# A third tile for keys, output weights loaded one group ahead, and one zero instead of a tile of zeros

## The chip, the core and the metric

The kernel runs on one core of one Trainium2 chip. The metric is the device time of one execution in microseconds (us). The names of the engines are those of the profile: PE multiplies matrices, DVE does elementwise work and scans, ACT evaluates functions, POOL does small elementwise work, SP issues transfers (DMA). Each engine takes its instructions in the order in which they were written into its queue; a scheduler wrote that order when the kernel was built, from the order of the program and an estimated timeline.

## The reference, cut to what matters

```python
# T = 2048 rows, D = 1024, 8 heads of 64, 8 gating groups of 64, D_FF = 4096
h = rmsnorm(x, norm_mix_g)
q, k, v, u, vg = split(h @ w_in)              # 5 x 512 columns
# stick-breaking attention, for each query t and key s < t (else 0):
z = q @ k.T / 8
a[t, s] = sigmoid(z[t, s]) * prod(1 - sigmoid(z[t, j]) for s < j < t)
a_out = a @ v
b_out = spatial_gating(gelu(u), gelu(vg), ...)
mix = concat(rmsnorm(a_out), rmsnorm(b_out))
x = x + mix @ w_out
h = rmsnorm(x, norm_mlp_g)
x = x + square(relu(h @ w_up)) @ w_down
return rmsnorm(x, norm_final_g)
```

## The kernel before

The 2048 rows are worked on in 4 chunks of 512 (`c` = 0 to 3). Every matrix product is made of three matmuls of split operands (`mm3`, L93 to L95: high x high, high x low, low x high); `split` (L85, L86) makes the two halves, a copy on ACT and a subtraction on DVE. Below, such a matmul is called a main matmul.

Attention is a generator of 320 steps. A unit is a chunk of queries, a head and a segment of 512 keys (1, 2, 3, 4 segments for chunks 0 to 3); it has 4 steps of 128 queries. A step has three parts. `weigh` makes the scores: two matmuls into `z` (three in a segment on the diagonal, where they are also narrower), two sigmoids on ACT (`kk`, `b`), a scan on DVE along the keys (`pr`, L385, or L382 on the diagonal) and a product on DVE (`b`, L386 or L383). `turn`, 5 steps later, transposes `b` on PE (`tr`, four transposes, or 4 to 1 in the steps of a diagonal unit) and splits the result into `aT`. `gather`, 2 steps after that, multiplies with the values (`av`, two matmuls); at the end of a head, `low` and `ao` add the halves, and every second head `ao` is stored to `a_d`.

Keys (`kt`, 2 tiles) and values (`vt`, 3 tiles) of a unit are loaded by SP at its first step; a load waits there until an earlier unit gives its tile back, and what stands behind it on SP waits as well.

The attention steps run beside other work: the projections of chunks 2 and 3, then for chunks 0, 1 and 2 the class `Out`, then `up_plain` (the up projection of chunks 0 and 1, between `Out(1)` and `Out(2)`) and `down_plain` (behind `Out(2)`). `together` sets how many steps go with a piece of main work. Attention of a chunk must have ended before its `Out` begins.

`Out` has three parts. `operands` loads the gating output (`b_d`, L499) and the attention output (`a_d`, L501), transposes the first on PE (L514), splits both, and sums squares of the second with 32 matmuls by a column of ones (L524, below called the ones). `product` has 192 main matmuls in 4 groups of 48 (`group(half, part, ...)`), each with a pair of weight tiles from `wo_d` (L532), and adds each result into rows of x (`ys`) on DVE (L555). `turn` normalises the rows (L574, L576) and transposes them (L581). The pair for group (0, 1) is loaded in `operands`; each other pair where its group begins:

```python
def group(half, part, m, rr):
    ws = self.ready.pop() if self.ready else self.weights(half, part)
```

The tiles named `t` come from one pool of 14 (`rm.t8`), which `Out`, `up_plain` and `down_plain` share. `zeros` is a tile of 513 columns of zeros: the scan adds it (L382, L385), and POOL copies from it into a part of `aT` (L401).

Of the kernel before, what the change touches and what calls it, by code (L numbers as in the profile page):

```python
# [8 lines left out]
F32 = mybir.dt.float32  # L9
F32R = mybir.dt.float32r  # L10
BF16 = mybir.dt.bfloat16
AF = mybir.ActivationFunctionType
ALU = mybir.AluOpType
# [3 lines left out]
P = 128  # L17
# [3 lines left out]
HD = 64  # L21
SBW = 512
DFF = 4096
TC = 512
# [10 lines left out]
def block_kernel(ctx: ExitStack, tc: tile.TileContext, x, x_t, gmix, w_in, ln_g, ln_b, sgw, sgb,  # L35
                 outg, w_out, gmlp, w_up, w_down, gfin, out):
    nc = tc.nc
# [34 lines left out]
    wo_d = dram.tile([2, 2, 2, P, 4, 512], F32, name="wo_d")  # L72
# [268 lines left out]
    def attention(cs):  # L341
# [4 lines left out]
        def weigh(u, tb):  # L346
# [4 lines left out]
            if tb == 0:  # L351
                kt = att.tile([P, 2, TC], F32R, name="kt", bufs=2)
# [4 lines left out]
                if diag:  # L357
                    qt = att.tile([P, TC], F32R, name="qt", bufs=2)
                    nc.sync.dma_start(qt.bitcast(F32), q_d[h].rearrange("x d t -> (x d) t")[:, tcs])
                    carry = [None] * NTB  # L360
# [20 lines left out]
            if diag:  # L381
                nc.vector.tensor_tensor_scan(pr[:, L - 1::-1], kk[:, L - 1::-1], zeros[:, :L], 1.0, ALU.mult, ALU.add)  # L382
                nc.vector.tensor_tensor(b[:, :L - 1], b[:, :L - 1], pr[:, 1:L], ALU.mult)  # L383
            else:
                nc.vector.tensor_tensor_scan(pr[:, ::-1], kk[:, ::-1], zeros, carry[tb], ALU.mult, ALU.add)  # L385
                nc.vector.tensor_tensor(b, b, pr[:, 1:TC + 1], ALU.mult)  # L386
# [3 lines left out]
        def turn(u, j):  # L390
# [8 lines left out]
            if t0 > TC - 2 * P:  # L399
                t0 = TC - 2 * P  # L400
                nc.gpsimd.tensor_copy(aT[:, :, t0:t0 + P], zeros[:, :2 * P].rearrange("p (a b) -> p a b", a=2))  # L401
# [4 lines left out]
        def gather(u, j):  # L406
# [14 lines left out]
            low = att.tile([HD, TC], F32, name="low", bufs=1)  # L421
            nc.scalar.activation(low, av[HD:2 * HD, :], AF.Copy)
            o0 = (h % 2) * HD
            nc.vector.tensor_tensor(ao[o0:o0 + HD, :], av[0:HD, :], low, ALU.add)
# [63 lines left out]
    class Out:  # L488
# [5 lines left out]
        def operands(self):  # L494
            rm, c = self.rm, self.c
            self.rbs = []
            self.ready = [self.weights(0, 1)]
# [31 lines left out]
        def weights(self, half, part):  # L529
            w = self.rm.pair([4, 512])  # L530
            for i in range(2):
                nc.sync.dma_start(w[i].bitcast(F32), wo_d[half, part, i])  # L532
            return w

        def product(self):
# [9 lines left out]
            def group(half, part, m, rr):  # L545
                ws = self.ready.pop() if self.ready else self.weights(half, part)
# [13 lines left out]
            yield from group(0, 1, self.bm, self.rbs)  # L560
            yield from group(0, 0, self.am, self.ras)
            yield from group(1, 1, self.bm, self.rbs)
            yield from group(1, 0, self.am, self.ras)
# [424 lines left out]
    with ExitStack() as es:  # L988
# [4 lines left out]
        zeros = att.tile([P, TC + 1], F32, name="zeros")  # L993
# [96 lines left out]
```

## Time and profile before

| what | value |
|---|---|
| time, median of 3 runs | 2500.56 us (2498.76 to 2502.59) |
| the profiled execution | 2500.81 us |
| its span, first to last instruction | 2499.1 us |
| mean granted clock of PE | 0.985 of full speed |
| busy PE, DVE, ACT, POOL | 97%, 67%, 48%, 13% of the span |

Busy is time in which an engine executes; the granted clock 1.0 is 2.4 GHz and 0.5 is 1.2 GHz, and a value between is a mean over a stretch in which both occurred. A window of the profile gives the busy time of each engine in a stretch of the span; what an engine lacks to the length of the window is its idle time there.

### The profile page before, as it was taken

The page shows a single profiled execution, that of the slowest core. Times are in us where ns is not written, and L with a number is a line of the kernel's source. Part 1 is how long each engine was busy: PE and PEld are TensorE (multiplying, and loading weights), DVE is VectorE, ACT ScalarE, POOL GpSimd, SP SyncE. Part 2 cuts the span into 40 slices and gives each one's busy share as a digit, 9 for nine tenths or more (in the row PEclk, how much of TensorE's full clock was granted, in tenths as well). Part 3 has the DMA queues.
Part 4 walks back from the last instruction along what each step waited for, and adds up shares of the span by engine and source line. Part 5 has one row for each costly group of instructions (what it writes and reads, how often), then busy time and mean ns, then how long its engine had stood idle before and what let it go on. Part 6 is the DMA issues. An engine that isn't in the chain of part 4 may idle for free.

```text
span 2499.1 us, 30545 instructions
## 1 busy us (share of the span) xinstructions
PE 2427.0 (97%) x11424; PEld 1986.8 (79%) x11424; DVE 1686.5 (67%) x2264; ACT 1197.9 (48%) x2004; POOL 322.1 (13%) x288
## 2 busy tenths in 40 slices
PE   8999999998899999999999899999999999899998
PEld 7888788886687888888877688888888888688886
DVE  4752678865957666666668878744686666577788
ACT  5433457553736655655655545322244444433333
POOL 1110011000100000000000000000123222224432
PEclk9999999998999999999989999999999999999999
DMA  9788977668644334433364543353533444744422
GB/s 378 295 303 280 316 256 247 200 217 282 199 148 143 119 125 131 122 115 111 124 257 170 176 130 113 105 197 126 211 118 139 155 146 163 260 182 153 168 101 101
DMA packets 161108, 455.00 MB, mean 182 GB/s; under 512 B 13376, under 2 KB 29760, under 8 KB 141504
## 3 DMA queue, kind: packets, MB, share of 16 engines
q1 hardware_dynamic: 150320, 417.39, 49.3%
q0 software_dynamic: 6336, 33.56, 3.3%
q10 hardware_dynamic: 4304, 2.10, 0.3%
q8 instruction: 90, 1.47, 0.2%
q14 instruction: 58, 0.48, 0.1%
HBM read 322.97 MB, written 130.02 MB: 181 GB/s over the span
## 4 chain that ended last, share of the span: by engine, by line
PE 83%; DVE 8%; DMA 4%; issue 3%; ACT 2%; POOL 0%; SPq 0%; DVEq 0%; POOLq 0%; ACTq 0%
PE mm L94 23%; PE mm L95 23%; PE mm L93 23%; PE tr L396 4%; PE av L414 2%; PE av L415 2%; PE z L370 2%; PE z L371 2%; DVE w L86 2%; DMA v_d<-qkv_st 1%; DVE pr L385 1%; DMA w_in<-wi_d 1%; PE mm L524 1%; DVE t L86 1%; DVE aT L86 1%
## 5 line engine op out<-in xcount | busy, mean ns | idle before, releaser
L93 PE MATMUL mm<-t,t 128*128 128x512 f32 x1280 | 503.7, 395 | 1.4 <-DVE t L86 1.4
L95 PE MATMUL mm<-t,t 128*128 128x512 f32 x1280 | 503.1, 393 | 0.0
L94 PE MATMUL mm<-t,t 128*128 128x512 f32 x1280 | 501.8, 392 | 0.0
L377 ACT ACTIVATE kk<-z,rq 128x512 f32<-128x512 f32 (+2 forms) x320 | 201.7, 631 | 289.0 <-PE z L371 177.0
L385 DVE TENSOR_TENSOR_SCAN pr<-kk,pr,zeros 128x513 f32<-128x513 f32 x192 | 246.6, 1285 | 119.1 <-ACT kk L377 118.7
L93 PEld LDWEIGHTS mm<-t,t 128*128 128x128 f32 x1280 | 242.3, 189 | 52.0 <-DVE t L86 1.9
L95 PEld LDWEIGHTS mm<-t,t 128*128 128x128 f32 x1280 | 241.7, 189 | 51.8
L94 PEld LDWEIGHTS mm<-t,t 128*128 128x128 f32 x1280 | 242.0, 189 | 50.1
L85 ACT ACTIVATE aT<-tr 128x512 fp32r<-128x512 f32 (+1 forms) x320 | 172.1, 541 | 100.2 <-PE tr L396 99.5
L86 DVE TENSOR_TENSOR aT<-tr,aT 128x512 fp32r<-128x512 f32 (+1 forms) x320 | 190.7, 599 | 25.3 <-ACT aT L85 25.2
L396 PE MATMUL tr<-ident,b 128*128 128x128 f32 x1088 | 180.9, 279 | 24.2 <-DVE aT L86 21.9
L379 ACT ACTIVATE b<-z,rq 128x512 f32<-128x512 f32 (+2 forms) x320 | 201.0, 629 | 2.8 <-PE tr L396 2.7
L85 ACT ACTIVATE t<-t 128x1024 fp32r<-128x1024 f32 x104 | 104.5, 1059 | 170.4 <-DMA t<-in_w_down 101.3
L94 PE MATMUL mm<-w,w 128*128 128x512 f32 x448 | 176.3, 393 | 8.8 <-DVE w L86 8.6
L396 PEld LDWEIGHTS tr<-ident,b 128*128 128x128 f32 x1088 | 133.2, 143 | 60.7 <-DVE aT L86 30.4
L95 PE MATMUL mm<-w,w 128*128 128x512 f32 x448 | 175.1, 391 | 0.0
L85 ACT ACTIVATE w<-raw 128x512 fp32r<-128x512 f32 (+1 forms) x135 | 106.7, 802 | 140.4 <-PE mm L95 130.7
L382 DVE TENSOR_TENSOR_SCAN pr<-kk,zeros 128x128 f32<-128x128 f32 (+3 forms) x128 | 104.4, 818 | 92.0 <-ACT kk L377 91.8
L86 DVE TENSOR_TENSOR w<-raw,w 128x512 fp32r<-128x512 f32 (+1 forms) x135 | 149.9, 1112 | 0.9 <-ACT w L85 0.4
L95 PE MATMUL mm<-t,w 128*128 128x512 f32 x380 | 150.3, 396 | 0.0
L93 PE MATMUL mm<-t,w 128*128 128x512 f32 x380 | 150.2, 395 | 0.0
L94 PE MATMUL mm<-t,w 128*128 128x512 f32 x380 | 150.2, 395 | 0.0
(215 smaller groups left out, 4730.8 us busy)
## 6 DMA issues: line engine op xcount, KB each, us to landing
w_in<-wi_d SPq DMA_DIRECT2D x40, 1024.0 KB, 8.5
kt<-k_d SPq DMA_DIRECT2D x160, 256.0 KB, 5.0
t<-wo_d SPq DMA_DIRECT2D x32, 1024.0 KB, 8.9
t<-in_w_down SPq DMA_DIRECT2D x28, 1024.0 KB, 7.1
raw<-s_d SPq DMA_DIRECT2D x28, 1024.0 KB, 4.8
wi_d<-w_in POOLq DMA_DIRECT2D x20, 1024.0 KB, 10.3
vt<-v_d SPq DMA_DIRECT2D x80, 256.0 KB, 2.7
t<-in_w_up SPq DMA_DIRECT2D x16, 1024.0 KB, 7.6
```

What stands on the lines that cost most here:

```text
L85: nc.scalar.activation(hi, src, AF.Copy)
L86: nc.vector.tensor_tensor(lo, src, hi.bitcast(F32), ALU.subtract)
L93: nc.tensor.matmul(ps, lh, rh, start=first, stop=False, skip_group_check=more)
L94: nc.tensor.matmul(ps, lh, rl, start=False, stop=False, skip_group_check=more)
L95: nc.tensor.matmul(ps, ll, rh, start=False, stop=last, skip_group_check=more)
L370: nc.tensor.matmul(z[:, :Z], ql, kt[:, 0, :Z], start=True, stop=False)
L371: nc.tensor.matmul(z[:, :Z], ql, kt[:, 1, :Z], start=False, stop=not diag)
L377: nc.scalar.activation(kk[:, :L], z[:, :L], AF.Sigmoid, scale=rq[:, 1, row:row + 1])
L379: nc.scalar.activation(b[:, :L], z[:, :L], AF.Sigmoid, scale=rq[:, 0, row:row + 1])
L382: nc.vector.tensor_tensor_scan(pr[:, L - 1::-1], kk[:, L - 1::-1], zeros[:, :L], 1.0, ALU.mult, ALU.add)
L385: nc.vector.tensor_tensor_scan(pr[:, ::-1], kk[:, ::-1], zeros, carry[tb], ALU.mult, ALU.add)
L396: nc.tensor.transpose(tr[:, tb * P:(tb + 1) * P], bs[tb][:, j * P:(j + 1) * P], ident)
```

## The change

Keys get three tiles instead of two. To make room, the tile of zeros becomes one column, which the scan and POOL read again and again, and the tile `low` goes: ACT copies the lower half of the sum straight to its place in `ao`, and DVE adds to it there. In `Out`, the weights of a group are loaded where the group before it begins, and each of these loads keeps its place in the order of the program on SP, so that it stands behind every transfer that the program issues earlier; before, the scheduler could move it ahead.

```diff
-                kt = att.tile([P, 2, TC], F32R, name="kt", bufs=2)
+                kt = att.tile([P, 2, TC], F32R, name="kt", bufs=3)
...
-                nc.vector.tensor_tensor_scan(pr[:, L - 1::-1], kk[:, L - 1::-1], zeros[:, :L], 1.0, ALU.mult, ALU.add)
+                nc.vector.tensor_tensor_scan(pr[:, L - 1::-1], kk[:, L - 1::-1], zeros.broadcast_to([P, L]), 1.0, ALU.mult, ALU.add)
...
-                nc.vector.tensor_tensor_scan(pr[:, ::-1], kk[:, ::-1], zeros, carry[tb], ALU.mult, ALU.add)
+                nc.vector.tensor_tensor_scan(pr[:, ::-1], kk[:, ::-1], zeros.broadcast_to([P, TC + 1]), carry[tb], ALU.mult, ALU.add)
...
-                nc.gpsimd.tensor_copy(aT[:, :, t0:t0 + P], zeros[:, :2 * P].rearrange("p (a b) -> p a b", a=2))
+                nc.gpsimd.tensor_copy(aT[:, :, t0:t0 + P], zeros.unsqueeze(2).broadcast_to([P, 2, P]))
...
-            low = att.tile([HD, TC], F32, name="low", bufs=1)
-            nc.scalar.activation(low, av[HD:2 * HD, :], AF.Copy)
             o0 = (h % 2) * HD
-            nc.vector.tensor_tensor(ao[o0:o0 + HD, :], av[0:HD, :], low, ALU.add)
+            nc.scalar.activation(ao[o0:o0 + HD, :], av[HD:2 * HD, :], AF.Copy)
+            nc.vector.tensor_tensor(ao[o0:o0 + HD, :], av[0:HD, :], ao[o0:o0 + HD, :], ALU.add)
...
-            self.ready = [self.weights(0, 1)]
+            self.ready = []
+            self.weights(0, 1)
...
-                nc.sync.dma_start(w[i].bitcast(F32), wo_d[half, part, i])
-            return w
+
+                tc.keep_in_program_order(nc.sync.dma_start(w[i].bitcast(F32), wo_d[half, part, i]))
+            self.ready.append(w)
...
-            def group(half, part, m, rr):
-                ws = self.ready.pop() if self.ready else self.weights(half, part)
+            def group(half, part, m, rr, then):
+                for hp in then:
+                    self.weights(*hp)
+                ws = self.ready.pop(0)
...
-            yield from group(0, 1, self.bm, self.rbs)
-            yield from group(0, 0, self.am, self.ras)
-            yield from group(1, 1, self.bm, self.rbs)
-            yield from group(1, 0, self.am, self.ras)
+            yield from group(0, 1, self.bm, self.rbs, [(0, 0)])
+            yield from group(0, 0, self.am, self.ras, [(1, 1)])
+            yield from group(1, 1, self.bm, self.rbs, [(1, 0)])
+            yield from group(1, 0, self.am, self.ras, [])
...
-        zeros = att.tile([P, TC + 1], F32, name="zeros")
+        zeros = att.tile([P, 1], F32, name="zeros")
```

With this the scheduler writes another order on all engines. Three places of it follow; a row is the line, the operation, what it writes and reads, and its shape, and `x2` stands for two such rows in a run. From L418 on the lines of the changed kernel have other numbers (L532 became L533, L555 became L558, L634 became L637).

First SP, where `up_plain` ends and `Out(2)` begins. Before (`t` are the pool's tiles, `act_d` takes the last results of the up projection):

```order
L356 DMA vt<-v_d 128x512
L354 DMA kt<-k_d 64x2x512 x2
L532 DMA t_11441<-wo_d 128x2048
L532 DMA t_11442<-wo_d 128x2048
L499 DMA t_11445<-b_d 128x4x512
L356 DMA vt<-v_d 128x512
L501 DMA t_11447<-a_d 128x4x512
L354 DMA kt<-k_d 64x2x512 x2
L634 DMA act_d_98<-t_11158 128x1024
L634 DMA act_d_99<-t_11158 128x1024
L356 DMA vt<-v_d 128x512
L354 DMA kt<-k_d 64x2x512 x2
```

Of the change:

```order
L356 DMA vt<-v_d 128x512
L354 DMA kt<-k_d 64x2x512 x2
L637 DMA act_d_98<-t_11132 128x1024
L356 DMA vt<-v_d 128x512
L637 DMA act_d_99<-t_11132 128x1024
L533 DMA t_11414<-wo_d 128x2048
L533 DMA t_11415<-wo_d 128x2048
L499 DMA t_11418<-b_d 128x4x512
L501 DMA t_11420<-a_d 128x4x512
L354 DMA kt<-k_d 64x2x512 x4
L359 DMA qt<-q_d 128x512
L356 DMA vt<-v_d 128x512
```

The two `wo_d` loads, `b_d` and `a_d` stood ahead of the last two stores to `act_d` and now stand behind both; four loads of `kt` stand behind them in a run.

Then DVE at the start of the product of `Out(2)`. Before (L555 adds a result of 12 main matmuls into `ys`; `SCALAR_TENSOR_TENSOR pr` is the scan; the other rows but L77 are attention's):

```order
L77 TENSOR_SCALAR ra_m<-mm 128x4
L555 SCALAR_TENSOR_TENSOR t_11573<-mm,rb,t_11573 128x512 x2
L555 SCALAR_TENSOR_TENSOR t_11575<-mm,rb,t_11575 128x512
L86 TENSOR_TENSOR aT<-tr,aT 128x512
L555 SCALAR_TENSOR_TENSOR t_11575<-mm,rb,t_11575 128x512
L385 SCALAR_TENSOR_TENSOR pr<-kk_1875,pr,zeros 128x513
L386 TENSOR_TENSOR b<-b,pr 128x512
L86 TENSOR_TENSOR aT<-tr,aT 128x512
L555 SCALAR_TENSOR_TENSOR t_11573<-mm,ra_r,t_11573 128x512
L382 SCALAR_TENSOR_TENSOR pr<-kk_1877,zeros 128x128
L383 TENSOR_TENSOR b<-b,pr 128x127
L86 TENSOR_TENSOR aT<-tr,aT 128x512
```

Of the change:

```order
L386 TENSOR_TENSOR b<-b,pr 128x512
L77 TENSOR_SCALAR ra_m<-mm 128x4
L558 SCALAR_TENSOR_TENSOR t_11546<-mm,rb,t_11546 128x512 x2
L558 SCALAR_TENSOR_TENSOR t_11548<-mm,rb,t_11548 128x512 x2
L558 SCALAR_TENSOR_TENSOR t_11546<-mm,ra_r,t_11546 128x512 x2
L558 SCALAR_TENSOR_TENSOR t_11548<-mm,ra_r,t_11548 128x512 x2
L558 SCALAR_TENSOR_TENSOR t_11546<-mm,rb,t_11546 128x512 x2
L558 SCALAR_TENSOR_TENSOR t_11548<-mm,rb,t_11548 128x512
L86 TENSOR_TENSOR aT<-tr,aT 128x384
L423 TENSOR_TENSOR ao<-av,ao 64x512
L558 SCALAR_TENSOR_TENSOR t_11548<-mm,rb,t_11548 128x512
L385 SCALAR_TENSOR_TENSOR pr<-kk_1879,pr,zeros 128x513
```

Eleven additions of the product now run without an attention step between them; before, one or more rows of attention stood behind the third and behind each later one.

Last DVE at the start of the product of `Out(0)`. Before:

```order
L77 TENSOR_SCALAR ra_m<-mm 128x4
L555 SCALAR_TENSOR_TENSOR t_5289<-mm,rb,t_5289 128x512 x2
L555 SCALAR_TENSOR_TENSOR t_5291<-mm,rb,t_5291 128x512 x2
L555 SCALAR_TENSOR_TENSOR t_5289<-mm,ra_r,t_5289 128x512 x2
L555 SCALAR_TENSOR_TENSOR t_5291<-mm,ra_r,t_5291 128x512 x2
L555 SCALAR_TENSOR_TENSOR t_5289<-mm,rb,t_5289 128x512 x2
L555 SCALAR_TENSOR_TENSOR t_5291<-mm,rb,t_5291 128x512
L385 SCALAR_TENSOR_TENSOR pr<-kk_1879,pr,zeros 128x513
L386 TENSOR_TENSOR b<-b,pr 128x512
L555 SCALAR_TENSOR_TENSOR t_5291<-mm,rb,t_5291 128x512
L385 SCALAR_TENSOR_TENSOR pr<-kk_1875,pr,zeros 128x513
L386 TENSOR_TENSOR b<-b,pr 128x512
```

Of the change:

```order
L385 SCALAR_TENSOR_TENSOR pr<-kk_1877,pr,zeros 128x513
L386 TENSOR_TENSOR b<-b,pr 128x512
L385 SCALAR_TENSOR_TENSOR pr<-kk_1879,pr,zeros 128x513
L86 TENSOR_TENSOR aT<-tr,aT 128x384
L386 TENSOR_TENSOR b<-b,pr 128x512
L423 TENSOR_TENSOR ao<-av,ao 64x512
L86 TENSOR_TENSOR aT<-tr,aT 128x256
L77 TENSOR_SCALAR ra_m<-mm 128x4
L558 SCALAR_TENSOR_TENSOR t_5276<-mm,rb,t_5276 128x512 x2
L558 SCALAR_TENSOR_TENSOR t_5278<-mm,rb,t_5278 128x512 x2
L558 SCALAR_TENSOR_TENSOR t_5276<-mm,ra_r,t_5276 128x512 x2
L558 SCALAR_TENSOR_TENSOR t_5278<-mm,ra_r,t_5278 128x512 x2
```

Four pairs of scan and product that stood among the additions (L385 and L386; two of the pairs are in the first excerpt) now stand ahead of the first addition, two of them in the second excerpt, and with them three rows of `aT`.

## Rows read from the trace of the kernel before

**Rows 1.** Part 1 of the page: busy us of each engine, share, instructions.

```profile
PE 2427.0 (97%) x11424; PEld 1986.8 (79%) x11424; DVE 1686.5 (67%) x2264; ACT 1197.9 (48%) x2004; POOL 322.1 (13%) x288
```

**Rows 2.** Waits of PE: total us, times, longest us.

```profile
PE tr L396 <- DVE aT L86: 21.9, 21, 3.7
PE av L414 <- DMA vt<-v_d: 1.7, 1, 1.7
PE z L370 <- DMA kt<-k_d: 0.4, 1, 0.4
```

**Rows 3.** Windows: length, busy of each engine, PEclk, DMA share, GB/s.

```profile
558.50:591.97 33.47, 23.48 (x123) 16.94 (x122) 28.95 (x49) 25.98 (x54) 3.33 (x5) 0.90 0.99 313
647.20:689.74 42.54, 31.25 (x162) 23.11 (x160) 42.01 (x65) 36.70 (x72) 5.72 (x7) 0.88 0.80 263
1276.00:1295.19 19.19, 15.49 (x74) 13.08 (x73) 17.57 (x23) 13.86 (x23) 0.00 (x0) 0.68 0.89 331
1295.19:1357.00 61.81, 61.81 (x293) 50.91 (x293) 39.53 (x56) 22.39 (x42) 3.42 (x4) 0.96 0.36 127
1357.00:1397.16 40.16, 28.26 (x146) 20.39 (x145) 37.44 (x51) 31.25 (x57) 2.81 (x3) 0.89 1.02 329
1397.16:1450.00 52.84, 52.84 (x241) 43.54 (x241) 38.13 (x47) 20.54 (x29) 0.00 (x0) 0.98 0.32 101
```

**Rows 4.** SP's issues in time order: start, us until issued.

```profile
650.70 0.43 SPq L499 DMA_DIRECT2D t<-b_d  x1
1251.30 0.42 SPq L499 DMA_DIRECT2D t<-b_d  x1
1269.24 7.12 SPq L634 DMA_DIRECT2D act_d<-t  x2
```

**Rows 5.** DVE by form: count, busy us, mean ns, idle before.

```profile
L385 DVE TENSOR_TENSOR_SCAN pr<-kk,pr,zeros 128x513 f32<-128x513 f32 x192 | 246.6, 1285 | 119.1 <-ACT kk L377 118.7
L386 DVE TENSOR_TENSOR b<-b,pr 128x512 f32<-128x512 f32 x192 | 132.0, 688 | 12.4 <-DVE pr L385 0.9
L86 DVE TENSOR_TENSOR aT<-tr,aT 128x512 fp32r<-128x512 f32 x224 | 152.0, 680 | 23.2 <-ACT aT L85 23.2
L86 DVE TENSOR_TENSOR aT<-tr,aT 128x384 fp32r<-128x384 f32 x32 | 17.4, 545 | 0.6 <-ACT aT L85 0.5
L86 DVE TENSOR_TENSOR aT<-tr,aT 128x256 fp32r<-128x256 f32 x32 | 13.2, 412 | 0.0
L424 DVE TENSOR_TENSOR ao<-av,low 64x512 f32<-64x512 f32 x32 | 21.7, 679 | 2.8 <-ACT low L422 2.2
L289 DVE TENSOR_TENSOR vn<-mm,sgb_t 128x256 f32<-128x256 f32 x24 | 8.9, 413 | 0.4 <-PE mm L286 0.4
```

**Rows 6.** DVE by line, the four widths of a line together.

```profile
L382 DVE TENSOR_TENSOR_SCAN pr<-kk,zeros 128x128 f32<-128x128 f32 (+3 forms) x128 | 104.4, 818 | 92.0 <-ACT kk L377 91.8
L383 DVE TENSOR_TENSOR b<-b,pr 128x127 f32<-128x127 f32 (+3 forms) x128 | 62.3, 489 | 9.6 <-ACT t L520 0.3
```

**Rows 7.** Chain that ended last, 645 to 700 us: start, us, what.

```profile
663.41 0.60 DVE b L386
664.01 0.60 DVE aT L86
664.61 1.19 DVE pr L385
```

**Rows 8.** PE in time order near 688 us: start, busy us.

```profile
688.02 0.40 PE L414 MATMUL av<-aT,vt 128*128 128x512 f32 x1
688.25 0.40 PE L370 MATMUL z<-kt,qt 128*128 128x512 f32 x1
688.49 0.39 PE L371 MATMUL z<-kt,qt 128*128 128x512 f32 x1
688.72 0.60 PE L396 MATMUL tr<-ident,b 128*128 128x128 f32 x4
689.07 0.47 PE L415 MATMUL av<-aT,vt 128*128 128x512 f32 x1
```

## The prediction

> **What bounds the kernel now.** Part 1 of the page comes first: PE is busy for 2427.0 of 2499.1 us, so some 72 us of idle PE is all that a better order could win, and whatever makes PE idle costs its full length [rows 1]. The waits of PE say who makes it idle. The longest wait among the attention steps is transposes for a split on DVE, 21.9 us; waits for loaded values come to 1.7 us, and for keys to 0.4 us, once [rows 2]. No row of that view has PE waiting for `wo_d`. So the two loads that the change speeds up stand in nobody's way.
>
> Next I looked at where PE is idle, by windows. Around each `Out` there is a stretch in which the program has no main matmuls ready and PE works through attention steps alone. I call it bare. There are four: ahead of the product of `Out(0)` (558.5 to 591.97 us), of `Out(1)` (647.2 to 689.74) and of `Out(2)` (1276 to 1295.19), and ahead of `down_plain` (1357 to 1397.16). In them PE is idle 9.99, 11.29, 3.70 and 11.90 us, together 36.9, while DVE is busy for 28.95 of 33.47, 42.01 of 42.54, 17.57 of 19.19 and 37.44 of 40.16 us [rows 3]. In a bare stretch DVE sets the pace. In the windows behind, where steps lie between main matmuls, PE is busy from end to end and DVE only in part: 39.53 of 61.81 us in the product of `Out(2)`, 38.13 of 52.84 at the start of `down_plain` [rows 3]. There a step costs PE's time for its own matmuls and DVE's part is free.
>
> **The third tile, the zeros, `low`.** An earlier load of keys can take away the 0.4 us, nothing more; I count 0, bounds -0.4 and 0 [rows 2]. The scan with one zero read again is not in the trace. The nearest row is L289, which reads a column again and again and takes 413 ns, against 412 ns for L86 of the same 256 columns with two full operands [rows 5]; so I take 0 for the scan, and a rival has the other value. POOL copies the same 256 columns as before, and POOL is 13% busy [rows 1]; 0, hidden behind the steps between turn and gather. Without `low`, ACT and DVE do the same two instructions for a head; only the wait for the store of `ao` moves from DVE to ACT. Bounds 0 and one such addition, 0.68 us, for a head that ends in a bare stretch [rows 5]; 0.
>
> **The weights and what moves with them.** `wo_d` loads keep their place on SP, and `b_d` and `a_d` follow them. Before, `b_d` for `Out(2)` was issued at 1251.30 us, while `up_plain` still ran; now it stands behind both last stores to `act_d`, which were issued from 1269.24 us until 7.12 us later [rows 4]. For `Out(1)` it was issued at 650.70 us [rows 4]; now it stands behind a key tile that needs the scores of attention step 108, ten steps into the bare stretch. Behind them four loads of keys stand in a run, as the order of SP shows, which the third tile allows. With the operands late, the scheduler lets more attention steps run first. Counted in PE's order, the scores of this many steps stand ahead of the first main matmul behind each bare stretch, before and now: 92 and 96; 115 and 118; 255 and 263; 282 and 287 (here ahead of the fourth main matmul, before the fourth having come 2 steps after the first). At the beginning of each stretch the counts agree, and they agree again when the product, or the first part of `down_plain`, is done. Twenty steps lose their cover of main matmuls.
>
> **Price on DVE.** DVE's order ahead of the first addition behind each stretch has, more than before: for `Out(0)` 4 scans, 4 products and splits of 512, 384 and 256 columns, 4 x 1.285 + 4 x 0.688 + 0.680 + 0.545 + 0.412 = 9.5 us; for `Out(1)` 3 scans, 5 products, splits of 3 x 512, 384 and 256 and one addition into `ao`, 3.86 + 3.44 + 2.04 + 0.96 + 0.68 = 11.0; for `Out(2)` 4 full scans, 4 diagonal ones at 0.818, 4 products at 0.489, 4 at 0.688 and 8 splits, 5.14 + 3.27 + 1.96 + 2.75 + 5.44 = 18.6; for `down_plain` 5 scans, 3 products and a split, 9.2 [rows 5, 6]. The sum is 48.2 us. Those means contain overlap with the next instruction: in the chain a product, a split and a scan follow each other in 0.60 + 0.60 + 1.19 = 2.39 us [rows 7], against 2.65 us by the means, 0.90 of it. That makes 43.4 us.
>
> Some of it fits into DVE's idle time in the four windows, 4.52 + 0.53 + 1.62 + 2.72 = 9.4 us [rows 3]. Much of that idle time is DVE waiting for its turn in a chain through PE and ACT, so I let half be filled, 4.7 us; bounds 0 and 9.4.
>
> **Price given back on PE.** The same steps no longer take PE time among the main matmuls. At full clock a 512-column attention matmul comes 0.23 to 0.24 us after the one before, and four transposes take 0.35 us [rows 8]. Moved, place by place, are 8, 6, 16 and 10 score matmuls (8 of the 16 are diagonal, some narrower; I take them all at 0.24 and leave out their four short masks), 6, 17, 32 and 4 transposes, and 0, 8, 15 and 2 value matmuls, counted in PE's order: 2.4 + 4.8 + 10.1 + 3.2 = 20.5 us back.
>
> **The sum.** 43.4 - 4.7 - 20.5 = +18.2 us. Its bounds: 43.4 - 9.4 - 20.5 = +13.5 and 48.2 - 20.5 = +27.7. The profiled execution took 2500.8 us, 1.7 more than its span and 0.2 more than the median of the runs, so the forecast is 2519 us, from 2514 to 2528.5. The granted clock is 0.68 to 0.89 in the bare stretches and 0.96 to 0.98 behind them [rows 3]: of the two levels the lower (1.2 GHz) is met there, after DVE has kept PE waiting. Longer bare stretches do not change what DVE needs, so I add nothing; main matmuls that start at the lower level are in both kernels.
>
> The Trainium skill, in Perfetto Trace Analysis, Optimization Strategy, says that a kernel whose most loaded engine changes over time may gain by interleaving its regimes. The windows agree (DVE full in the bare stretches, PE full behind them), and this change separates the regimes further; the page gives no size, so by it the time would rise by an amount that only the rows tell.
>
> **Rivals.** *The loads themselves come too late.* For `Out(1)`, ten steps at 2.39 us put the issue of `b_d` at 671 us or later. In the old run the first main matmul came 43.5 us after that issue (694.2 against 650.70). If all of that were in series, it would come at 714.7, where the sum above has 694.2 + 0.90 x 11.0 - 0.3 = 703.8: 11 us more, 2530. Against it: that time was filled with attention on DVE, not with waiting.
>
> *The pulled steps hide behind the ones.* The 32 one-column matmuls L524 need nothing of DVE, and DVE works through what is queued. In the third window PE is busy with them to its end at 1295.19 while DVE has 1.62 us left [rows 3]. If in each of the four places another 4.5 us of pulled DVE work ran behind PE's own, 18 us would be covered: 2501, no change. Against it: transposes ahead of the ones wait for DVE, and most of the pulled work is theirs.
>
> *The scan gets cheaper with one column of zeros.* The other side: a scan costs 1285 ns for 513 columns, a product of two tiles 688 [rows 5]. If the second operand is what costs the difference, each scan saves up to 0.5 us on average, and the bare stretches hold 72 steps now (13, 18, 6 and 15 before, counted in PE's order, and the 20): -36 us, 2483. It decides from 0.25 us a scan on (18.2 / 72). Against it: L289 saves nothing.
>
> *More tiles remove the gaps.* Repeated gaps in front of the same instructions would mean that tiles of keys run out; with a third all 36.9 us of idle PE in the bare stretches [rows 3] would go, and the steps pulled ahead would be the ones that now can run: 2464. Against it: the row for keys has 0.4 us [rows 2]. The Trainium skill, in Perfetto Trace Analysis, Optimization Strategy, has this reading of a gap that keeps coming back; the waits here do not bear it out.
>
> **How the numbers follow.** Chances: the forecast 0.68, loads too late 0.10, hidden behind the ones 0.14, cheaper scan 0.05, more tiles 0.03. Within 0.2% (5 us) is about what a measurement of this kernel can tell from no change. Slower by more than that: 0.68 + 0.10 = 0.78; same 0.14; faster 0.08. The range holds the forecast's bounds and the late loads; as the cases below them hold 0.22, it takes in the upper part of the hidden case too: 2505 to 2531.
>
> **What would show it.** In the changed profile the four bare stretches are longer by some 6, 10, 16 and 7 us with DVE busy throughout, the products behind them shorter by some 2, 5, 10 and 3; PE's waits for DVE's splits grow by 10 to 20 us in all; the waits for keys were and stay under 1 us; scans take 1.28 us. The prediction is wrong if DVE shows idle time in longer bare stretches (loads late), if the stretches did not grow, or if the mean of L385 moved.

## The result and the profile after

The changed kernel took 2520.3 us, median of 4 runs (2515.7 to 2523.5), against 2499.7 us (2498.1 to 2502.6) for the kernel before on the same chip: 1.008 times, 95% interval 1.0061 to 1.0098. The forecast was 2519. The profiled execution took 2515.7 us, 14.9 more than the profiled one of before; it is the fastest of the four, so what is read from it place by place adds up to 14.9 and not to the 20.6 of the medians.

The page's part 1, the line that answers to [rows 1]:

```profile
PE 2433.5 (97%) x11424; PEld 1987.6 (79%) x11424; DVE 1684.1 (67%) x2264; ACT 1198.5 (48%) x2004; POOL 325.1 (13%) x288
```

PE is busy for 6.5 us more with the same number of instructions, and the span grew by 14.9, so 8.4 us are idle time of PE. The mean granted clock of PE is 0.984, before 0.985. PE's waits, as in [rows 2] (total, times, longest):

```profile
PE tr L396 <- DVE aT L86: 30.4, 32, 2.2
...
PE z L370 <- ACT b L379: 6.9, 8, 1.9
...
PE av L414 <- ACT t L85: 2.1, 1, 2.1
...
PE mm L95 <- DVE w_in L86: 0.9, 1, 0.9
...
PE mm L514 <- DMA t<-b_d: 0.6, 1, 0.6
...
PE z L370 <- DMA kt<-k_d: 0.3, 1, 0.3
```

Transposes wait 8.5 us more for DVE's splits, in 32 places instead of 21; the forecast had 10 to 20 us. Keys cost 0.3 us instead of 0.4, and `b_d`, which is issued later, 0.6. The windows that answer to [rows 3], each from the same point of the program to the same point (length, busy of each engine, PEclk, DMA share, GB/s); second and fourth are the products of `Out(0)` and `Out(1)`, which stood at 49.83 and 56.68 us:

```profile
562.78:598.96 36.18, 26.73 (x137) 18.97 (x136) 35.24 (x57) 30.76 (x62) 2.55 (x6) 0.91 0.97 293
602.70:649.98 47.28, 47.28 (x211) 39.22 (x211) 17.32 (x28) 3.52 (x9) 2.12 (x3) 0.97 0.50 178
649.98:701.89 51.91, 40.03 (x193) 30.00 (x192) 51.33 (x77) 43.51 (x84) 9.22 (x8) 0.80 0.71 199
706.28:757.74 51.46, 51.46 (x229) 42.52 (x230) 22.47 (x33) 7.16 (x15) 2.11 (x3) 0.95 0.48 158
1283.06:1318.83 35.77, 26.43 (x143) 20.22 (x142) 34.60 (x51) 28.92 (x55) 2.80 (x4) 0.91 0.93 315
1318.83:1369.49 50.66, 50.66 (x225) 41.69 (x226) 21.07 (x30) 9.75 (x18) 2.51 (x4) 0.96 0.34 132
1369.49:1413.74 44.25, 30.89 (x168) 22.17 (x166) 43.18 (x60) 37.05 (x67) 3.55 (x3) 0.96 0.96 307
```

The bare stretches (first, third, fifth, seventh) are longer by 2.7, 9.4, 16.6 and 4.1 us than in [rows 3], with DVE busy to within 1.2 us of each; the products behind are shorter by 2.6, 5.2 and 11.2. SP's issues that answer to [rows 4] (start, us until issued):

```profile
674.14 0.44 SPq L499 DMA_DIRECT2D t<-b_d  x1
...
1283.49 0.38 SPq L637 DMA_DIRECT2D act_d<-t  x1
1283.92 1.50 SPq L533 DMA_DIRECT2D t<-wo_d  x2
1285.47 0.48 SPq L499 DMA_DIRECT2D t<-b_d  x1
```

`b_d` for `Out(2)` goes out at 1285.47 us, behind the last store to `act_d`, when the last main matmul of `up_plain` had ended at 1280.76; before it went out at 1251.30, 22 us ahead of that end. For `Out(1)` it goes out at 674.14 instead of 650.70; 2.8 us of that, and 7.1 of the difference at `Out(2)`, are what the changed kernel had lost up to there. The scan did not change, as DVE by form shows ([rows 5] has 1285 ns too):

```profile
L385 DVE TENSOR_TENSOR_SCAN pr<-kk,pr,zeros 128x513 f32<-128x513 f32 x192 | 246.5, 1285 | 114.2 <-ACT kk L377 113.8
```

One place was not in the forecast. The last projection matmul ends at 561.69 us instead of 557.41, 4.3 us late before any of the four stretches begins. PE in time order there (start, busy, idle time before and what ended it):

```profile
270.50 0.38 PE L370 MATMUL z<-kt,qt 128*128 128x256 f32 x1 [1.86 <-ACT b L379]
...
271.81 0.69 PE L396 MATMUL tr<-ident,b 128*128 128x128 f32 x2 [0.74 <-DVE b L383]
...
273.53 0.80 PE L93 MATMUL mm<-hT,w_in 128*128 128x512 f32 x1 [0.47 <-DVE gelu_t L205]
```

and ACT just before:

```profile
268.88 0.63 ACT L85 ACTIVATE qkv_st<-gelu_t 128x512 fp32r<-128x512 f32 x1 [9.31 <-DMA k_d<-qkv_st]
```

where the kernel before has

```profile
266.32 0.63 ACT L85 ACTIVATE qkv_st<-gelu_t 128x512 fp32r<-128x512 f32 x1 [5.95 <-DMA k_d<-qkv_st]
```

ACT stood 9.31 us in front of a write to `qkv_st` until a store to `k_d` gave the tile back (5.95 us before), and the sigmoids of two steps were queued behind it; PE wanted their score tiles. SP shows what went out just ahead of these stores. In the changed kernel a further pair of key loads stands there:

```profile
255.49 1.36 SPq L354 DMA_DIRECT2D kt<-k_d  x2
...
258.97 2.80 SPq L208 DMA_DIRECT2D k_d<-qkv_st  x4
```

In the kernel before, that pair stands behind the stores:

```profile
258.00 3.20 SPq L208 DMA_DIRECT2D k_d<-qkv_st  x4
...
269.03 1.29 SPq L354 DMA_DIRECT2D kt<-k_d  x2
```

### The profile page after: what moved, and what is told of

Same layout as the page of the kernel before. It is cut to its first block, busy times and chain, and to the rows that moved or that the text cites. A ratio compares the mean times of both kernels' runs of the same rounds, so it can differ in the third digit from the quotient of the medians.

```text
span 2514.0 us, 30563 instructions
## 1 busy us (share of the span) xinstructions
PE 2433.5 (97%) x11424; PEld 1987.6 (79%) x11424; DVE 1684.1 (67%) x2264; ACT 1198.5 (48%) x2004; POOL 325.1 (13%) x288
## 4 chain that ended last, share of the span: by engine, by line
PE 83%; DVE 9%; DMA 4%; issue 2%; ACT 1%; POOL 0%; SPq 0%; DVEq 0%; POOLq 0%; ACTq 0%
PE mm L94 23%; PE mm L95 23%; PE mm L93 23%; PE tr L396 4%; PE av L415 2%; PE av L414 2%; PE z L370 2%; PE z L371 2%; DVE w L86 2%; DVE pr L385 1%; DMA v_d<-qkv_st 1%; DVE aT L86 1%; DVE t L86 1%; PE mm L524 1%; DVE b L386 1%
## 5 line engine op out<-in xcount | busy, mean ns | idle before, releaser
L385 DVE TENSOR_TENSOR_SCAN pr<-kk,pr,zeros 128x513 f32<-128x513 f32 x192 | 246.5, 1285 | 114.2 <-ACT kk L377 113.8
L401 POOL CAST aT<-zeros 128x256 fp32r<-128x256 f32 x32 | 25.8, 807 | 982.2 <-PE av L415 939.9
L86 DVE TENSOR_TENSOR t<-t,t 128x1024 fp32r<-128x1024 f32 x104 | 123.6, 1226 | 41.0 <-PE mm L94 20.7
L95 PE MATMUL mm<-t,w 128*128 128x512 f32 x380 | 150.3, 396 | 0.0
## 6 DMA issues: line engine op xcount, KB each, us to landing
t<-wo_d SPq DMA_DIRECT2D x32, 1024.0 KB, 10.1
wi_d<-w_in POOLq DMA_DIRECT2D x20, 1024.0 KB, 10.6
```

The lines of the kernel that those rows point to most:

```text
L86: nc.vector.tensor_tensor(lo, src, hi.bitcast(F32), ALU.subtract)
L95: nc.tensor.matmul(ps, ll, rh, start=False, stop=last, skip_group_check=more)
```

## The experiments

Each was timed beside the kernel before on the same chip, whose median lay at 2500.2 us for the first four kernels below, at 2499.6 for the next three and the higher share, and at 2500.2 for the other four. Runs of one kernel spread by 4 to 12 us, so medians are compared; a stretch of a single profile carries some 3 us of chance (last section). The scores that the expectations count are those that stand ahead of the first main matmul behind each bare stretch (before 92, 115, 255, 282; where the fourth is counted up to the first main matmul of `down_plain`, and not to the fourth, it is 280 before).

**One column of zeros, no `low`, nothing else.**

```diff
-        zeros = att.tile([P, TC + 1], F32, name="zeros")
+        zeros = att.tile([P, 1], F32, name="zeros")
...
-            low = att.tile([HD, TC], F32, name="low", bufs=1)
-            nc.scalar.activation(low, av[HD:2 * HD, :], AF.Copy)
+            nc.scalar.activation(ao[o0:o0 + HD, :], av[HD:2 * HD, :], AF.Copy)
```

> Of the change only the one column of zeros and the end of low; keys in two tiles, output weights as before. The scores ahead of the first main matmul behind each bare stretch are 92, 115, 255, 282 again, as in the kernel before. Theory (time follows the steps that lose their cover): no change, 2500 us within 3, and PE's gaps of the projections as before. Rival (the one column or the sum written in two steps into ao costs something, for instance the 4.3 us that the changed kernel loses in the projections): 2503 to 2505, with the loss ahead of 562 us in the span.

Measured 2500.6 us, ratio 1.0001 (0.9992 to 1.0011). These edits cost nothing and bring nothing that the runs can tell (the interval spans 5 us); the rival of a cheaper scan falls here as it did in the row of L385.

**The third key tile with the old code for the weights.**

```diff
-                kt = att.tile([P, 2, TC], F32R, name="kt", bufs=2)
+                kt = att.tile([P, 2, TC], F32R, name="kt", bufs=3)
```

> The third key tile with the zeros and low that make room for it; output weights as before. Scores ahead of the first main matmul: 96, 114, 255, 286, so 4 steps more in front of Out(0) and 4 more in front of down_plain, none in front of Out(1) and Out(2). Theory (steps without cover): by the terms on record Out(0) and down_plain give 0.90 x (9.5 + 9.2) - 2.4 - 3.2 = 11.2, less half of DVE's idle time there (3.6), +7.6; with the 4.3 us seen in the projections 2512, without them 2508. By what the trace after showed at these places (projections +4.3, Out(0) -1.5, down_plain +2.4): 2505. Rival (the queueing of weights does it all): 2500.

Measured 2506.7 us, 1.0022 (1.0013 to 1.0031). That is near 2505, the value by what the trace after showed, and below 2508 and 2512, the values by the terms on record. The last projection matmul ends 6.4 us late, and of the 6.8 us that the profiled span is longer only 0.4, on balance, arose behind it. The projections, 200 to 300 us, in this kernel:

```profile
200.00:300.00 100.00, 95.53 (x435) 76.91 (x435) 38.05 (x67) 34.26 (x68) 4.37 (x14) 0.97 0.92 289
```

and in the kernel before:

```profile
200.00:300.00 100.00, 99.22 (x470) 80.17 (x469) 42.49 (x73) 38.04 (x76) 5.41 (x15) 1.00 0.93 303
```

PE has 3.7 us more idle time, is granted 0.97 of full speed on the mean, so that it meets the lower of its two clock levels (1.2 GHz), and gets 35 instructions less done. The 7.6 us for 8 steps more ahead of `Out(0)` and `down_plain` did not come.

**Only the weights, with their place on SP kept.**

```diff
-                nc.sync.dma_start(w[i].bitcast(F32), wo_d[half, part, i])
+                tc.keep_in_program_order(nc.sync.dma_start(w[i].bitcast(F32), wo_d[half, part, i]))
...
-            yield from group(0, 1, self.bm, self.rbs)
+            yield from group(0, 1, self.bm, self.rbs, [(0, 0)])
```

> Only the output weights one group ahead with their place kept; two key tiles, the tile of zeros and low as before. Scores ahead of the first main matmul: 92, 116, 260, 280, with as many transposes ahead of the products of Out(1) and Out(2) as in the changed kernel (339 and 858, the changed one has 339 and 860; before 322 and 828). Theory: Out(1) and Out(2) lose as in the trace after, +4 and +4 to +5, nothing elsewhere: 2508, at least 2505. Rival (the third key tile does it all): 2500.

Measured 2510.1 us, 1.0033 (1.0020 to 1.0046). SP in this kernel:

```profile
671.11 0.43 SPq L500 DMA_DIRECT2D t<-b_d  x1
...
1283.07 0.52 SPq L500 DMA_DIRECT2D t<-b_d  x1
```

The two loads are as late as in the changed kernel. From the start of the turn of `Out(0)` to that of `Out(1)` the profile lost 4.1 us, in `Out(2)` 3.2; in the projections it gained 0.3. In the bare stretch behind the turn of `Out(0)` PE does 156 instructions in 42.78 us instead of 129 in 33.64, and in the product 234 in 51.60 instead of 260 in 56.68:

```profile
660.37:703.15 42.78, 32.05 (x156) 25.21 (x157) 41.40 (x62) 31.07 (x59) 3.18 (x6) 0.80 0.84 252
703.15:754.75 51.60, 51.60 (x234) 42.62 (x235) 23.87 (x35) 9.42 (x19) 2.12 (x3) 0.97 0.41 142
```

An instruction of attention cost 9.14 / 27 = 0.34 us in the bare stretch and 5.08 / 26 = 0.20 between main matmuls. Of the 9.14 us, 0.7 belong to the 32 ones at the end of the stretch, which were granted 0.65 of full speed here and 0.79 before; without them it is 0.31.

**The changed kernel with `b_d` and `a_d` issued ahead of the first pair of weights.**

```diff
-            self.weights(0, 1)
             st = rm.t8([4, SBW])
...
             nc.sync.dma_start(at, a_d[:, c * TC:(c + 1) * TC].rearrange("(n p) t -> p n t", p=P))
+            self.weights(0, 1)
```

> The changed kernel with one thing moved: in operands the pair of weights (0, 1) is issued behind b_d and a_d instead of ahead of them, still in program order. Scores ahead of the first main matmul: 94, 115, 255, 286; transposes 254, 326, 828, 932 (changed kernel 271, 339, 860, 932). Theory (b_d behind the pinned weights is what pulls steps ahead): as the kernel with the third key tile alone or a little less, 2504 to 2508. Rival (the weights one group ahead cost by their own transfers and waits): 2515 to 2520 as in the changed kernel.

Measured 2507.2 us, 1.0024 (1.0013 to 1.0034): 13 us of the 20 are gone with the order of three transfers. `b_d` goes out at 658.18 and 1257.02 us. What is left arises in the projections: their last matmul ends 6.9 us late, the profiled span is 6.3 longer.

**The changed kernel with the third key tile held back.** The tile becomes one of its own and is written by POOL at step 75, so no keys can be loaded into it earlier.

```diff
-                kt = att.tile([P, 2, TC], F32R, name="kt", bufs=3)
+                if u >= 20 and u % 3 == 2:
+                    kx = att.tile([P, 2, TC], F32R, name="kx", bufs=1)
+                else:
+                    kx = att.tile([P, 2, TC], F32R, name="ky", bufs=2)
+                kt = kx
...
+            if u == 18 and tb == 3:
+                ke = att.tile([P, 2, TC], F32R, name="kx", bufs=1)
+                nc.gpsimd.tensor_copy(ke[:, 0, 0:1], pr[:, 0:1])
```

> The changed kernel with the third key tile held back: it is a tile of its own that comes free only at attention step 75, when the projections are nearly done. In the projections SP's order is that of the kernel before again (keys behind the stores to k_d); the scores ahead of the first main matmul are those of the changed kernel, 96, 118, 263, 287. Theory (the third tile lets keys be loaded ahead of the stores to k_d, and ACT, which waits for these stores, makes PE wait): the loss of the projections goes, 4.3 us by the profile of the changed kernel and up to 6.9 by the other kernels with three tiles, and the rest stays: 2514 to 2516, with the last w_in matmul ending at 557 to 558 us instead of 561.7. Rival (the loss of the projections comes from elsewhere, the run differs by chance there): 2520.

Measured 2516.8 us, 1.0070 (1.0057 to 1.0082). The projections are back where they were:

```profile
200.00:300.00 100.00, 98.59 (x467) 79.70 (x466) 42.76 (x73) 37.94 (x75) 4.99 (x15) 1.00 0.94 298
```

Their last matmul ends at 556.8 us, and ACT's wait for the store is 7.45 us. So at its place the loss is the third tile's early load. All other profiles bear this out: the last projection matmul ends at 555 to 559 us in the nine kernels with two key tiles and at 561 to 564 in the four with three, and ACT's wait for that store is 5.7 to 7.3 us in the nine and 8.9 to 10.1 in the four. In the total no gain is shown: it is 3.5 us less by the medians, but the intervals overlap, and the two profiled spans agree (2514.2 and 2514.0).

**Two key tiles, weights kept in order, operands first.** The same move of `self.weights(0, 1)`, made in the kernel that has only the new code for the weights.

> Two key tiles, the tile of zeros and low as before; output weights one group ahead in program order, but the pair (0, 1) issued behind b_d and a_d. Scores ahead of the first main matmul: 90, 115, 255, 280 (before: 92, 115, 255, 282 with the fourth counted two matmuls later). Theory: with the third key tile gone the 6.9 us of the projections go too, and two steps more are covered at Out(0) and at down_plain; 2498 to 2501, no change from before or a little faster. Rival (pinned weights cost by themselves): 2503 or more.

Measured 2504.1 us, 1.0019 (1.0011 to 1.0028). This is the rival's value, but the trace does not give its reason; the theory missed by 3 us or more. By the profile the loss is in `Out(0)`: two steps fewer stand ahead of its product, and the product is longer by 4.8 us (54.60 instead of 49.83, with 243 instructions of PE instead of 225), but the stretch ahead is as long as before (39.91 from the last projection to the first main matmul, before 39.96). Of that stretch the part ahead of the ones is 1.3 us shorter (33.23 instead of 34.56), and the ones are 1.3 us longer (6.68 us at a granted clock of 0.50, before 5.40 at 0.63). PE also waits for loads there:

```profile
575.05 1.53 PE L515 MATMUL mm<-ident,t 128*128 128x128 f32 x12 [3.11 <-DMA t<-b_d]
...
588.08 0.76 PE L414 MATMUL av<-aT,vt 128*128 128x512 f32 x1 [2.65 <-DMA vt<-v_d]
```

So loads have a part in the length of this stretch; in the kernel before, PE's waits there were for DVE but for 1.7 us for `vt`, 0.4 for `kt` and 0.5 for ACT. The kernel with 52 products left out, below, bears on it.

**Every third product of the bare steps on POOL.**

```diff
-                nc.vector.tensor_tensor(b, b, pr[:, 1:TC + 1], ALU.mult)
+                ve.tensor_tensor(b, b, pr[:, 1:TC + 1], ALU.mult)
...
+            i = u * NTB + tb
+            bare = i in range(79, 92) or i in range(97, 115) or i in range(249, 255) or i in range(267, 282)
+            ve = nc.gpsimd if bare and i % 3 == 1 else nc.vector
```

> The kernel before, with one thing changed: of the steps that run in the four bare stretches (79 to 91, 97 to 114, 249 to 254, 267 to 281), every third takes its product b times pr on POOL instead of DVE, 18 products in all. Theory (DVE sets the pace in the bare stretches): 18 x 0.60 us of DVE time leave them, so up to 10.8 us less, 2490 to 2495, and PE's waits for DVE's splits fall from 22 us by as much. Rival (the steps' own chain through PE, ACT and DVE sets the pace, or POOL's product takes as much from DVE as it relieves it): 2500 or more.

Measured 2502.5 us, 1.0013 (1.0004 to 1.0022). No gain, rather a small loss. This alone would have spoken against DVE as the one that sets the pace, so the next kernels take the work away without giving it to POOL.

**The same 18 products left out; all 52 left out.** The second has no `i % 3 == 1`.

```diff
+                if not bare:
+                    nc.vector.tensor_tensor(b, b, pr[:, 1:TC + 1], ALU.mult)
```

> The kernel before without the 18 products b times pr that stood on POOL in the kernel with products on POOL; nothing takes their place, so for these 18 steps the scores are not multiplied by the product of the keys passed. The same steps stand ahead of the main matmuls as there (92, 113, 255, 280). Theory (DVE sets the pace in the bare stretches, and POOL's slower product in the chain of a step ate the gain): 18 x 0.60 = up to 10.8 us less, 2490 to 2494. Rival (the pace is set by something else, the chain of a step through PE and ACT, and less work on DVE is worth nothing): 2498 to 2503.

> The kernel before without the products b times pr of all 52 steps that run in the four bare stretches (so for these steps the scores are not multiplied by the product of the keys passed). Theory (DVE sets the pace): up to 52 x 0.60 = 31 us less; as DVE has 9.4 us of idle time there and ACT, busy 25.98 of 33.47 and 36.7 of 42.54 us, becomes the next bound, 2476 to 2486. Rival (chain): 2496 or more.

Measured 2494.4 us, 0.9976 (0.9965 to 0.9986), and 2489.0 us, 0.9954 (0.9942 to 0.9967). Less work on DVE does shorten the time, by 5.8 and 11.2 us, but by 0.32 and 0.22 us a product, not by 0.60; the second is above the bounds of the theory. The order changed too: in all three kernels two steps fewer stand ahead of the product of `Out(1)` (113 instead of 115), so the comparison with the kernel before is not of the products alone. Between the last two kernels the counts agree, and there 34 products more gave 5.4 us, 0.16 each. DVE's busy time in the profiles fell by 8.2 and 26.0 us. The page's part 1 of the kernel with 18 left out:

```profile
PE 2421.5 (97%) x11424; PEld 1983.5 (80%) x11424; DVE 1678.3 (67%) x2246; ACT 1198.0 (48%) x2004; POOL 321.5 (13%) x288
```

and of the kernel with 18 on POOL:

```profile
PE 2434.2 (97%) x11424; PEld 1993.4 (80%) x11424; DVE 1685.2 (67%) x2246; ACT 1200.1 (48%) x2004; POOL 344.5 (14%) x306
```

DVE's same 2246 instructions take 6.9 us longer beside 23 us of POOL. That is little more than chance: the profiles with 2264 instructions on DVE, in several orders, lie between 1683.6 and 1689.3 us. The Trainium skill, in Perfetto Trace Analysis, Optimizing Scalar/DVE Operations, warns that POOL and DVE share a read port, so that moving work between them may not help; the time of this kernel agrees, 2502.5 us against 2494.4 without these products, though no run shows the port.

With all 52 left out, this is what PE waits for ahead of `Out(0)`:

```profile
578.25 1.53 PE L518 MATMUL mm<-ident,t 128*128 128x128 f32 x12 [1.77 <-DMA t<-b_d]
586.44 0.55 PE L370 MATMUL z<-kt,qt 128*128 128x256 f32 x1 [4.96 <-DMA kt<-k_d]
```

and these are two of its windows, ahead of the ones of `Out(0)` and from the turn of `Out(0)` to the ones of `Out(1)`:

```profile
556.44:591.45 35.01, 25.01 (x131) 18.64 (x129) 25.25 (x39) 27.02 (x55) 2.68 (x5) 0.87 0.96 295
...
648.98:686.21 37.23, 29.43 (x165) 22.51 (x163) 34.38 (x50) 34.84 (x70) 4.96 (x7) 0.91 0.81 267
```

At `Out(0)`, where the order is that of the kernel before, DVE has 9.8 us idle and the stretch is no shorter (34.56 us before): now loads set it, with the DMA engines 96% busy. At `Out(1)` the stretch went from 42.54 to 37.23 us, two steps fewer included, and DVE and ACT are now both busy for all but 3 us; that ACT is the next bound is read from this, not tried.

**A higher share of attention in `Out(0)` and `Out(1)`.**

```diff
-    R_A, R_O, R_U = 1.0, 0.5, 0.49
+    R_A, R_O, R_U = 1.0, 0.7, 0.49
```

> The kernel before, with R_O at 0.7 instead of 0.5: more attention steps are written between the main matmuls of Out(0) and Out(1). Scores at the start of the bare stretch ahead of Out(1) and at its end: 104 and 116 instead of 97 and 115, so 6 steps of it gain cover; ahead of Out(2) 264 and 270 (before 249 and 255, as many), ahead of down_plain 26 to 28 steps instead of 25 to 27. Theory (a step without cover costs DVE's 2.39 us, a covered one PE's 1.2): 6 x 1.2 = 7 us less at Out(1) and 1 to 2 more at down_plain, 2495. Rival (steps cost the same wherever they stand): 2500.

Measured 2499.4 us, 1.0003 (0.9994 to 1.0013): the rival's value. The steps did move; no gain came that the runs can tell. The product of `Out(0)` took 58.24 us instead of 49.83 for 44 instructions of PE more, as expected for covered steps:

```profile
596.88:655.12 58.24, 58.24 (x269) 47.69 (x270) 36.00 (x51) 21.32 (x40) 3.72 (x5) 0.96 0.46 150
```

but the turn behind it, which also needs DVE, took 18.78 us instead of 13.38, to its last transposes. From there to the first main matmul of `Out(1)` 10.6 us were saved (23.04 instead of 33.64), and 8.4 and 5.4 had been spent in the product and the turn.

**The changed kernel without the kept order.**

```diff
-                tc.keep_in_program_order(nc.sync.dma_start(w[i].bitcast(F32), wo_d[half, part, i]))
+                nc.sync.dma_start(w[i].bitcast(F32), wo_d[half, part, i])
```

> The changed kernel without the call that keeps the loads of output weights in program order; they are still written one group ahead, and the scheduler may move them. Scores ahead of the first main matmul: 96, 114, 255, 286, as in the kernel with the third key tile and the old code for the weights. Theory (the kept order costs, writing the loads a group earlier costs nothing): as that kernel, 2505 to 2508, so 13 us below the changed kernel. Rival (the place one group ahead costs by itself): 2512 or more.

Measured 2505.5 us, 1.0024 (1.0014 to 1.0034), like the kernel with the third key tile alone. One call is worth some 15 us by the medians. With it gone the operands go out early again:

```profile
654.12 0.43 SPq L499 DMA_DIRECT2D t<-b_d  x1
...
1258.08 0.51 SPq L499 DMA_DIRECT2D t<-b_d  x1
```

**Eight steps early, no transfer's order changed by hand.**

```diff
+        for _ in range(8):
+            next(side)
         o = Out(2, rm)
```

> The kernel before with 8 attention steps called between up_plain and Out(2); no load of keys, weights or operands is changed. Scores ahead of the first main matmul: 260 at Out(2) (before 255), 290 at down_plain (280), and in PE's instructions of attention 33 more ahead of Out(2)'s product and 48 more ahead of down_plain's first main matmul. Theory (a step costs more without cover): by what the changed kernel showed at these places, 16.58 - 11.15 = 5.4 us net for 68 such instructions at Out(2), 0.08 us each, and 2.4 us for 21 at down_plain, 0.11 each, so +2.6 and +5.5: 2508. Rival (late operands cost, and steps ahead of them only fill the time): 2500.

Measured 2508.1 us, 1.0030 (1.0018 to 1.0041), as the theory had it. The profiled execution, the fastest of six, lost 5.7 us from the end of `up_plain` to the end of the span, and had won 2.4 ahead of it, where the counts are those of the kernel before. `b_d` goes out 22.4 us ahead of the end of `up_plain`, as before, and PE waits for no load in the stretch behind. So steps pulled ahead cost by themselves, without a late load.

No version that does the whole work was faster than the kernel before; the closest are the one with one column of zeros and the one with the higher share.

## Why the prediction was right, and where it was not

The change splits into two losses. The third key tile costs 6.5 us (or 5.3, by the kernel without the kept order), and the kept order of the weights 9.9 with two key tiles and some 14 with three. Tried one by one they come to 16.4 of the 20.6 us, and whether the rest is chance or comes of having both is open. Zeros and `low` cost nothing, and neither does the place one group ahead by itself, as the kernel without the kept order (2505.5 us) is no slower than the one with the third tile alone (2506.7).

| place | forecast | profile |
|---|---|---|
| projections | 0 | +4.3 |
| to the turn of `Out(0)` | 0.90 x 9.5 - 2.3 - 2.4 = +3.9 | -1.5 |
| to the turn of `Out(1)` | 0.90 x 11.0 - 0.3 - 4.8 = +4.8 | +4.1 |
| `up_plain` | 0 | +0.2 |
| to the turn of `Out(2)` | 0.90 x 18.6 - 0.8 - 10.1 = +5.8 | +5.4 |
| from there to the end | 0.90 x 9.2 - 1.4 - 3.2 = +3.7 | +2.4 |
| sum | +18.2 | +14.9 |

In the forecast's own terms, by the windows: DVE's busy time in the four stretches grew by 38.4 us for a forecast of 43.4, 5.6 us of it filled idle time for 4.7, and the main matmuls behind gave back 20.6 for 20.5. Not in the forecast were 4.3 us in the projections, 0.2 in `up_plain` and 1.7 fewer in the ones of `Out(0)` and `Out(1)`. Of the signs that were named, DVE was busy throughout, the products became shorter, keys were waited for less than 1 us and the scan kept its time; the stretches grew by 2.7, 9.4, 16.6 and 4.1 us for 6, 10, 16 and 7, and the waits for DVE's splits by 8.5 for 10 to 20.

*What bounds the kernel.* In part. Transposes wait for DVE in more places, and the two kernels with products left out show that DVE's time in the bare stretches counts, but at a half to a quarter of its price: ACT is close behind it at `Out(1)`, and at `Out(0)` loads hold the stretch as soon as DVE has less to do. "In a bare stretch DVE sets the pace" holds ahead of `Out(1)` and `Out(2)`, where the stretches grew as DVE's busy time did (9.4 us for 9.3, 16.6 for 17.0), and less at the others (2.7 for 6.3, 4.1 for 5.7); it does not say what taking work away is worth.

*The kept order pulls steps ahead.* Shown: `b_d` goes out 23 and 34 us later, the stretches ahead of `Out(1)` and `Out(2)` grow and the products behind them shrink, and both undoings, the call and the order of three transfers, give 13 to 15 us back. The terms for `Out(1)` and `Out(2)` were right to 0.7 us in this profile. At `Out(2)` this is luck in part: the stretch ahead of the ones grew by 18.2 us for a forecast of 15.9, the ones took 5.04 us instead of 6.68 at a higher clock (0.68 for 0.50), and the product gave back 11.2 for 10.1. The forecast added nothing for the clock.

*The third tile.* "I count 0, bounds -0.4 and 0" was wrong. The forecast looked for what a new tile would let PE do sooner, and not at what SP would issue sooner in a stretch where the DMA engines are over 90% busy. An extra load of keys stands ahead of the stores to `k_d`, ACT waits longer for these stores, and PE for ACT. That the early load does it is shown by the kernel that holds the tile back; that it does so by sharing the DMA engines with the store is read from the order and the waits, not tried. The term for the four steps pulled ahead of `Out(0)`, which stay ahead in the kernel with the third tile alone, was mis-sized by 5.4 us. DVE's busy time in that stretch grew by 6.3 us and not by 8.6, 3.6 of it and not 2.3 filled idle time, the product gave back 2.6 for 2.4, and the ones took 3.74 us at a granted clock of 0.93 instead of 5.40 at 0.63. This last is chance: there they take 3.8 to 6.9 us in kernels with as many steps ahead as before, and 3.7 to 5.9 in those with four more. The two errors, +4.3 and -5.4, nearly cancelled, and that was luck.

*The rivals.* Loads too late: PE waited 0.6 us for `b_d` in the changed kernel, the first main matmul of `Out(1)` came 32.1 us after the issue of `b_d` and not 43.5, and the eight early steps cost the same kind of price with no late load. Steps hidden behind the ones: at `Out(0)` the pulled steps cost nothing on balance, but not in this way, as DVE did 3.61 us of work in the window of the ones and before 3.68; at the others the stretches grew. Cheaper scan: no, 1285 ns in both. Removed gaps: no; the Trainium skill's reading of gaps that keep coming back (Perfetto Trace Analysis, Optimization Strategy) did not apply, and a third tile made the kernel slower. In the same section of Perfetto Trace Analysis, the Trainium skill's advice to interleave regimes agrees with the eight early steps, which separated them and cost 7.9 us, while interleaving more than the kernel before, by the higher share, gave nothing that the runs can tell.

*Left open.* By its sum of places the profile gives 14.9 us; why the other three runs took 4.5 to 7.8 us more is not in any trace here. PE's busy time grew by 6.5 us with as many instructions; how much of that is the clock was not separated. Two key tiles with kept weights and the operands first still cost 4.5 us, for which no run gives the reason.

## What to carry to other kernels

A load kept in program order also holds back everything behind it on its queue: before pinning one, look at what is issued next and who needs it. A further buffer lets a load go out earlier; here, with the DMA engines over 90% busy, a store whose tile someone waited for then came later. So "nobody waits for this tile" bounds what it can gain, not what it can cost. Before pricing work by the busiest engine of a stretch, ask what else would end that stretch: ahead of `Out(0)` thirteen products less on DVE shortened nothing, as loads were next.

## What the runs showed of the hardware

The same instructions got different clocks. From the last main matmul of `up_plain` to the first of the product of `Out(2)`, in the kernel before:

```profile
1273.70:1295.19 21.49, 17.79 (x91) 15.13 (x91) 18.63 (x23) 16.13 (x26) 0.00 (x0) 0.71 0.80 296
```

and in the kernel with one column of zeros, which has as many scores, transposes and value matmuls there:

```profile
1275.27:1293.71 18.44, 14.22 (x92) 11.92 (x91) 16.98 (x21) 16.14 (x26) 0.00 (x0) 0.91 0.80 272
```

The second is 3.05 us shorter. The difference lies in the last 32 matmuls of PE, the ones, which come without a pause after a part that takes 14.8 us in both. In the kernel before:

```profile
1288.51:1295.19 6.68, 6.68 (x33) 6.68 (x33) 5.17 (x7) 1.35 (x3) 0.00 (x0) 0.50 1.02 425
```

and in the other:

```profile
1290.09:1293.71 3.62, 3.62 (x34) 3.62 (x33) 3.52 (x5) 1.35 (x3) 0.00 (x0) 0.96 1.03 428
```

At the lower of the two clock levels (0.50, 1.2 GHz) the ones take 6.68 us, almost wholly at the higher one (0.96) 3.62. Of the same matmuls ahead of other products, windows show 3.50 us at 1.00, 3.74 at 0.93, 5.40 at 0.63 and 6.68 at 0.50. Between `Out(0)` and `Out(1)` the two kernels above differ the other way (0.82 and 33.64 us, 0.76 and 35.55). So PE, and not only DVE, has a part in the length of a bare stretch, and a difference of under 3 us in one stretch of one profile is no finding.
